# A streaming-encoder layer on one core: the second MLP product as seven half-size products, with weight sums made in DRAM

## The chip, the core and the metric

The kernel runs on one core of a Trainium2 chip. The engines are PE (matmuls), DVE, ACT and POOL (elementwise work, POOL only on SBUF) and SP, whose queue issues most transfers; sixteen DMA engines move the data of all queues. The metric is the time of one execution on the device in microseconds (us), as a median over runs.

## The reference, cut to what matters

One layer over 512 tokens and 16 meta tokens, width 1024, float32. The front computes an RWKV-7 branch and a forgetting-attention branch, gates them and projects the sum; then comes the MLP, which the change is about:

```python
h = h + (merged @ w_o[l]).astype(h.dtype)
z = rmsnorm(h, norm_mlp[l])
h = h + (jnp.square(jax.nn.relu(z @ w_up[l])) @ w_down[l]).astype(h.dtype)
return h[:, N_META:]
```

`z` is 512 x 1024 (the meta tokens are dropped by then), `w_up` 1024 x 4096, `w_down` 4096 x 1024.

## The kernel before

**Precision.** Every float32 operand of a large matmul is split into a high part (a cast to fp32r on ACT) and a low part (a subtraction, on DVE or POOL). A product is three passes: high by high, high by low, low by high (`passes`, line 259).

**Weights.** `load_h` (line 226) loads 128 x 512 floats, 256 KB, into a buffer `wraw` through SP's queue, casts it to `whi` on ACT (line 232) and subtracts to `wlo` (line 233). There are four buffers of each kind. `load_w` (line 236) is two such loads. The projections of the front have their own copy of this in `fetch` and `convert` (lines 430 and 438), with the subtraction on POOL (line 444).

**The front** (to about 450 us in the profile) is made of streams: the recurrence (`recurrent`, `chain`), attention, its features, and 40 projection blocks of u = rmsnorm(h) (`projections`, line 448). `Turns` (line 147) keeps a model of the time, `Clock`, and asks each stream in order of its rank for the time from which it can go on; the first that is due within `ROOM` of its rank writes its next instructions. This fixes the order on PE alone (`manual_schedule` at line 998). On the other engines and in the queues the compiler orders the instructions, by their place in the code and by when they are ready. Line 402, `act(gf, gf, AF.Tanh, scale=0.5)`, is one of the last steps before the streams start. The 16 gate blocks are projected at the lowest rank, written to DRAM (line 484) and read back at line 1028.

**The middle** (450 to 572 us): the output projections with the gates, `w_o`, the residual `hres` (4 blocks of 128 tokens by 1024), the second norm, and z transposed and split into `zhi` and `zlo`. The weights of the first two up blocks are loaded early into `we`, in the memory of `y_rw` and `y_fx`.

**The MLP** (from line 1106) goes over the 4096 hidden columns in two halves. In each half, 16 up blocks of 128 columns are computed: `up_part` writes 24 matmuls of 512 columns into a PSUM bank `po`, `up_evac` makes Relu on ACT (line 1122), squares on DVE (line 1124), casts to `fhi` (1125) and subtracts to `flo` (1126). The first three blocks of the first half are computed in two parts, since the tokens of z come in order. Then, for each half of the 1024 output columns, four banks `pd` gather 16 hidden blocks: every loaded block of `w_down` (128 x 512) serves four token blocks in three passes, 12 matmuls (line 1150). DVE adds each bank to `hres` (line 1153), and behind the second half the result is stored (line 1155).

Of the kernel before, what the change touches and what calls it, by code (L numbers as in the profile page):

```python
# [9 lines left out]
F32 = mybir.dt.float32  # L10
# [11 lines left out]
S = 512  # L22
# [3 lines left out]
HT = T // 2  # L26
KB = 8
CDEC = math.exp(-0.5)


C_MU = 0
# [28 lines left out]
class Clock:  # L60
# [35 lines left out]
    def read(self):  # L96

        new = self.nc.cur_bb.bb.instructions[self.seen:]
        self.seen += len(new)
        for x in new:  # L100
            outs = [o.bass_ap for o in x.outs if hasattr(o, "bass_ap")]
            ins = [o.bass_ap for o in x.ins if hasattr(o, "bass_ap")]
            if not outs:
                continue
            for o in outs:
                t = o.tensor
                if hasattr(t, "cap_key") and t.name not in self.free:
                    ring, n = self.rings.setdefault(str(t.cap_key).rsplit("_", 2)[0], []), t.tag_meta.bufs
                    self.free[t.name] = self.last(ring[-n]) if len(ring) >= n else 0.0
                    ring.append(t.name)  # L110
            names = [a.tensor.name for a in ins]
            out = outs[0].tensor.name
            eng = str(x.engine).split(".")[-1]

            def cols(a):
                return math.prod(n for _, n in a.ap[1:])
            deps = max([self.w.get(n, 0.0) for n in names] + [self.free.get(out, 0.0)])
            if eng == "PE":
                n = max(cols(outs[0]), 64)
# [27 lines left out]
class Turns:  # L147
# [37 lines left out]
def kernel(ctx, tc, ht, x, win, par, cst, gain, lora, wout, wo, wup, wdn, out, dbg=None):  # L185
# [73 lines left out]
    def passes(w, x):  # L259
        return ((w[0], x[0]), (w[0], x[1]), (w[1], x[0]))  # L260

    yp = ctx.enter_context(tc.tile_pool(name="yp", bufs=1))
    gates_d = [dr.tile([128, S], F32, name=f"gd{i}") for i in range(16)]

    with ExitStack() as st:
        up = st.enter_context(tc.tile_pool(name="up", bufs=1))
# [132 lines left out]

        lf, gf = (x[:, :T] for x in lfs)  # L400
        act(lf[:64], lf[:64], AF.Tanh)
        act(gf, gf, AF.Tanh, scale=0.5)
# [45 lines left out]
        def projections(total):  # L448
            fetched, done = None, 0
            while done < total:  # L450
                if fetched is None:
                    yield lambda: 0.0 if jobs else math.inf
                    fetched = fetch(jobs.pop(0))
                cur = convert(*fetched)
                fetched = fetch(jobs.pop(0)) if jobs else None
                while cur is not None:
                    (_, _, _, begin, parts, ev, need), w = cur
                    nxt = convert(*fetched) if fetched else None
                    fetched = fetch(jobs.pop(0)) if jobs else None
# [645 lines left out]

    with ExitStack() as st:
        dp = st.enter_context(tc.tile_pool(name="dp", bufs=1))
        for hh in range(2):
            fhi = dp.tile([128, 16, S], F32R, name="fhi")
            flo = dp.tile([128, 16, S], F32R, name="flo")  # L1110
            F = (fhi, flo)

            def up_part(w, po, t0, t1):
                n = 0
                for k in range(KB):
                    for a, b in passes(wk(w, k), Z):
                        mm(po[:, t0:t1], a, b[:, k, t0:t1], start=n == 0, stop=n == 23)  # L1117
                        n += 1

            def up_evac(b_, po):  # L1120
                r = dp.tile([128, 512], F32, name="r", bufs=2)
                act(r, po, AF.Relu)
                s2 = dp.tile([128, 512], F32, name="s2", bufs=2)
                V.scalar_tensor_tensor(s2, po, 0.0, r, ALU.max, ALU.mult)
                A.copy(fhi[:, b_, :], s2)
                V.tensor_tensor(flo[:, b_, :], s2, fhi[:, b_, :].bitcast(F32), ALU.subtract)

            first = 0
            if hh == 0:
# [4 lines left out]
                for b_ in range(3):  # L1134
                    up_part(ws[b_], pos[b_], 256, 512)
                    up_evac(b_, pos[b_])
                first = 3
            for b_ in range(first, 16):
                w = load_w(wup[16 * hh + b_])
                po = ppo()  # L1140
                up_part(w, po, 0, 512)
                up_evac(b_, po)
            for ch in range(2):
                pd = [ppd() for i in range(4)]
                for b2 in range(8):
                    w = load_w(wdn[hh, ch, b2])
                    for i, b1 in [(i, b1) for b1 in range(2) for i in range(4)] if b2 < 7 else [(i, b1) for i in range(4) for b1 in range(2)]:
                        b_ = 2 * b2 + b1
                        for n, (a, b) in enumerate(passes(F, w[b1])):
                            mm(pd[i], a[:, b_, 128 * i:128 * i + 128], b, start=b_ == 0 and n == 0, stop=b_ == 15 and n == 2)  # L1150
                for i in range(4):
                    hr = hres[:, i, 512 * ch:512 * ch + 512]
                    V.tensor_tensor(hr, hr, pd[i], ALU.add)
                    if hh == 1:
                        nc.sync.dma_start(out[128 * i:128 * i + 128, 512 * ch:512 * ch + 512], hr)


def host_layout(x, meta, norm_mix, w_in, b_gate, b_f, tm_mu, w0, w_lora_up, a0, a_lora_up, g_lora_up, k_k, k_a, r_k,
# [74 lines left out]
```

## Time and profile before

| | |
|---|---|
| median of 3 runs | 928.7 us (923.4 to 930.36) |
| span of the profiled execution | 921.7 us, 15446 instructions; its own time over all isn't listed beside the span |
| PE busy | 872.5 us (95%), mean granted clock 0.983 |
| DVE, ACT, POOL busy | 523.7 (57%), 424.9 (46%), 159.9 us (17%) |
| transfers | 83.30 MB, HBM read 75.99 MB, written 6.31 MB |

The span goes from the first to the last instruction. A busy PE is not PE at its peak, since matmuls overlap. In the lists of groups a row has the line, engine and operation, what is written from what, shape and count; then the busy time and the mean duration in ns of one; then the idle time of the engine just before, with what ended most of it. In a timeline a row begins with the start and the duration in us. A row of waits has who waited for whom, the total in us, how often, and the longest. A row of DMA issues ends with the KB of each and the median us from issue to landing.

### The profile page before, as it was taken

How to read it: one execution, taken by the hardware profiler on the slowest of the kernel's cores; microseconds unless marked ns; L12 is line 12 of the kernel's file. 1: busy time of each engine (PE TensorE's matmuls, PEld its weight loads, DVE VectorE, ACT ScalarE, POOL GpSimd, SP SyncE). 2: the span in 40 equal slices, each digit the busy share in tenths (PEclk: the TensorE clock that was granted, in tenths of full speed). 3: DMA queues.
4: the chain of work that ended last, by engine and by line, in shares of the span. 5: the costliest groups of instructions: out<-in, count | busy, mean ns of one | idle time of the engine just before them, and what ended most of it. 6: DMA issues, size and time to landing. Idle time of an engine off the chain costs nothing.

```text
span 921.7 us, 15446 instructions
## 1 busy us (share of the span) xinstructions
PE 872.5 (95%) x5964; PEld 709.4 (77%) x5964; DVE 523.7 (57%) x1052; ACT 424.9 (46%) x887; POOL 159.9 (17%) x145
## 2 busy tenths in 40 slices
PE   6589898999998999999989999999999999999998
PEld 4587785768896777676768878988888888888886
DVE  7966885465887893565387664454423245452322
ACT  7755352686465533674465553344322234442221
POOL 4253433123343352112102100000000000000000
PEclk9889998999999999999989999999999999999999
DMA  6121204022111142211266540132323232322331
GB/s 207 46 71 47 69 27 132 25 71 70 50 46 59 47 133 70 69 60 47 69 229 205 183 160 1 58 103 92 101 94 101 94 102 93 100 95 94 123 116 57
DMA packets 45449, 83.30 MB, mean 90 GB/s; under 512 B 5048, under 2 KB 6200, under 8 KB 45376
## 3 DMA queue, kind: packets, MB, share of 16 engines
q1 hardware_dynamic: 45376, 82.32, 26.8%
q8 instruction: 47, 0.77, 0.3%
q14 instruction: 26, 0.21, 0.1%
HBM read 75.99 MB, written 6.31 MB: 89 GB/s over the span
## 4 chain that ended last, share of the span: by engine, by line
PE 76%; DVE 15%; DMA 3%; ACT 3%; issue 2%; POOLq 0%; POOL 0%; SPq 0%; DVEq 0%; ACTq 0%
PE po L1117 19%; PE pd L1150 19%; PE pj L472 18%; PE po L1083 2%; PE po L1034 2%; PE pw L824 2%; PE psc L576 1%; PE py L621 1%; DVE tmp L806 1%; DMA wraw<-in_wup 1%; DVE AX L818 1%; DVE xt L373 1%; PE pbt L772 1%; DVE AX L807 1%; DMA wraw<-in_win 1%
## 5 line engine op out<-in xcount | busy, mean ns | idle before, releaser
L233 DVE TENSOR_TENSOR wlo<-wraw,whi 128x512 fp32r<-128x512 f32 x148 | 107.0, 724 | 171.6 <-ACT whi L232 170.1
L232 ACT CAST whi<-wraw 128x512 fp32r<-128x512 f32 x152 | 93.8, 620 | 190.4 <-PE pd L1150 109.6
L472 PE MATMUL pj<-uhi,whi 128*128 128x264 f32 (+1 forms) x480 | 168.5, 351 | 9.5 <-DVE orr L301 4.7
L472 PE MATMUL pj<-uhi,wlo 128*128 128x264 f32 (+1 forms) x480 | 156.3, 326 | 0.0
L472 PE MATMUL pj<-ulo,whi 128*128 128x264 f32 (+1 forms) x480 | 156.3, 326 | 0.0
L444 POOL TENSOR_TENSOR wlo<-wraw,whi 128x512 fp32r<-128x512 f32 x80 | 109.1, 1367 | 216.8 <-ACT whi L443 201.4
L472 PEld LDWEIGHTS pj<-uhi,whi 128*128 128x128 f32 x480 | 92.4, 192 | 30.6 <-issue 10.9
L1150 PE MATMUL pd<-whi,fhi 128*128 128x512 f32 x256 | 99.6, 389 | 0.0
L1150 PE MATMUL pd<-wlo,fhi 128*128 128x512 f32 x256 | 99.6, 389 | 0.0
L1150 PE MATMUL pd<-whi,flo 128*128 128x512 f32 x256 | 99.6, 389 | 0.0
L472 PEld LDWEIGHTS pj<-uhi,wlo 128*128 128x128 f32 x480 | 92.6, 193 | 7.2
L472 PEld LDWEIGHTS pj<-ulo,whi 128*128 128x128 f32 x480 | 92.7, 193 | 4.3
L1117 PE MATMUL po<-zhi,whi 128*128 128x512 f32 (+1 forms) x248 | 94.8, 382 | 0.0
L1117 PE MATMUL po<-zlo,whi 128*128 128x512 f32 (+1 forms) x248 | 94.8, 382 | 0.0
L1117 PE MATMUL po<-zhi,wlo 128*128 128x512 f32 (+1 forms) x248 | 94.8, 382 | 0.0
L443 ACT CAST whi<-wraw 128x512 fp32r<-128x512 f32 x80 | 49.4, 618 | 51.9 <-PE pj L472 27.5
L1150 PEld LDWEIGHTS pd<-whi,fhi 128*128 128x128 f32 x256 | 48.0, 188 | 10.1
L1150 PEld LDWEIGHTS pd<-wlo,fhi 128*128 128x128 f32 x256 | 48.0, 188 | 10.0
L1150 PEld LDWEIGHTS pd<-whi,flo 128*128 128x128 f32 x256 | 48.0, 188 | 9.9
L1117 PEld LDWEIGHTS po<-zlo,whi 128*128 128x128 f32 x248 | 46.6, 188 | 9.1
L1117 PEld LDWEIGHTS po<-zhi,whi 128*128 128x128 f32 x248 | 46.6, 188 | 9.0
L1117 PEld LDWEIGHTS po<-zhi,wlo 128*128 128x128 f32 x248 | 46.6, 188 | 9.0
(279 smaller groups left out, 1455.6 us busy)
## 6 DMA issues: line engine op xcount, KB each, us to landing
wraw<-in_win SPq DMA_DIRECT2D x84, 256.0 KB, 2.6
wraw<-in_wup SPq DMA_DIRECT2D x64, 256.0 KB, 2.6
wraw<-in_wdn SPq DMA_DIRECT2D x64, 256.0 KB, 2.6
gd<-gt SPq DMA_DIRECT2D x16, 256.0 KB, 2.1
wraw<-in_wout SPq DMA_DIRECT2D x16, 256.0 KB, 3.3
gl<-gd SPq DMA_DIRECT2D x16, 256.0 KB, 3.1
wraw<-in_wo SPq DMA_DIRECT2D x16, 256.0 KB, 3.2
xt<-in_ht SPq DMA_DIRECT2D x8, 264.0 KB, 4.7
```

Source lines behind the costliest of these rows:

```text
L232: A.copy(hi, raw)
L233: low.tensor_tensor(lo, raw, hi.bitcast(F32), ALU.subtract)
L373: V.scalar_tensor_tensor(xt[t][:, k, :], xt[t][:, k, :], pr[:, C_GN + k:C_GN + k + 1], rss[t], ALU.mult, ALU.mult)
L443: A.copy(hi, raw)
L444: G.tensor_tensor(lo, raw, hi.bitcast(F32), ALU.subtract)
L472: mm(po, a, b[:, k, a0:a1], start=n == 0, stop=n == 23)
L576: mm(sc, q[hs, 128 * i:128 * i + 128], k[hs, a:b], start=True, stop=True)
L824: mm(ps_[hs, n - b0, :], lhs(n)[hs], rhs(n)[hs], start=True, stop=True)
L1034: mm(po, a, b[:, k, :], start=n == 0, stop=n == 11)
L1083: mm(po, a[:, k, 128 * i:128 * i + 128], b[:, k, :], start=n == 0, stop=n == 23)
L1117: mm(po[:, t0:t1], a, b[:, k, t0:t1], start=n == 0, stop=n == 23)
L1150: mm(pd[i], a[:, b_, 128 * i:128 * i + 128], b, start=b_ == 0 and n == 0, stop=b_ == 15 and n == 2)
```

## The change

The second product F W (F: 512 x 4096, the squared Relu; W = `w_down`) is cut into 2 x 2 quadrants: F by token halves and by hidden blocks of even and odd number, W by those hidden blocks and by halves of the output columns. Strassen's scheme in Winograd's form computes it with seven products of quarter size in place of eight. It needs four sums of quadrants of F (s1 to s4), four of W, and sums of the results.

- The sums of W, `tsum`, four tensors of 2048 x 512 in DRAM, are made by DMAs: 16 copies of 1 MiB issued from ACT's queue and 16 adding DMAs of 1 MiB issued from POOL's. They are written as a new stream, `weight_sums`, of rank 9 in `Turns`, with due times of 50 us and 11 us more for each step; the copies are put behind line 402 (`opened`). `Clock` leaves them out of its model. t1 = B11 + B12, t3 = B12 + B22, t2 = B22 + t1, t4 = B21 + t2.
- The hidden dimension is worked through in three slices of 6, 6 and 4 pairs of blocks (`SLICES`). Up blocks are evacuated to a tile `R` in the memory of `y_rw` and `y_fx`; after each pair, POOL makes the four sums of 256 columns, and one cast and one subtraction of 7 x 256 columns make the pair's left factors.
- In each slice follow seven products. Each loads one 128 x 512 block per pair, from `wdn` or `tsum`, and uses it in 6 matmuls (two token blocks, three passes). Two products stay in PSUM over all slices (`x6`, `x7`, the four `pd` banks); two are gathered in SBUF (`v1`, `v5`); three are added to `hres` in each slice. In the last slice the sums over `v1`, `v5`, `x6`, `x7` follow on POOL and DVE.
- On the host, `w_down` is laid out in its four quadrants.

```diff
+SLICES = (6, 6, 4)
...
+            if out.startswith("tsum"):
+                continue
...
-    ROOM = {0: 0.0, 1: 0.8, 2: 1.5, 3: 1.5, 4: 2.5, 8: 0.5}
+    ROOM = {0: 0.0, 1: 0.8, 2: 1.5, 3: 1.5, 4: 2.5, 8: 0.5, 9: 0.0}
...
+    tsum = [dr.tile([2048, 512], F32, name=f"tsum{i}") for i in range(4)]
...
-        act(gf, gf, AF.Tanh, scale=0.5)
+        opened = act(gf, gf, AF.Tanh, scale=0.5)
...
+        def weight_sums():
+            def part(t, c):
+                return t[512 * c:512 * c + 512].rearrange("(a b) c -> a (b c)", b=4)
+            t1, t2, t3, t4 = tsum
+            b11, b12, b22, b21 = (wdn[i] for i in range(4))
+            steps = []
+            for c in range(4):
+                for dst, src in ((t1, b11), (t3, b12), (t2, b22), (t4, b21)):
+                    steps.append((dst, src, c, False))
+                for dst, src in ((t1, b12), (t3, b22), (t2, t1), (t4, t2)):
+                    steps.append((dst, src, c, True))
+            for n, (dst, src, c, adds) in enumerate(steps):
+                yield lambda: 50.0 + 11.0 * n
+                if adds:
+                    nc.gpsimd.dma_start(part(dst, c), part(src, c), accum_op=ALU.add, max_dma_last_dim=8192)
+                else:
+                    after(nc.scalar.dma_start(part(dst, c), part(src, c), max_dma_last_dim=8192), opened)
+        turns.add(9, weight_sums())
...
-        for hh in range(2):
-            fhi = dp.tile([128, 16, S], F32R, name="fhi")
...
+        def left_factors(fhi, flo, j, R):
+            a11, a12, a22, s1, s2, s3, s4, a21 = (R[:, i, :] for i in range(8))
+            G.tensor_tensor(s1, a22, a21, ALU.subtract)
+            G.tensor_tensor(s3, a11, a21, ALU.subtract)
+            G.tensor_tensor(s2, a11, s1, ALU.add)
+            G.tensor_tensor(s4, s2, a12, ALU.subtract)
+            A.copy(fhi[:, j], R[:, :7])
+            V.tensor_tensor(flo[:, j], R[:, :7], fhi[:, j].bitcast(F32), ALU.subtract)
...
+        for n_pairs in SLICES:
+            fhi = dp.tile([128, max(SLICES), 7, 256], F32R, name="fhi")
...
+            def product(x, left, right, start, stop):
+                for j in range(0, n_pairs, 2):
+                    r0 = 128 * (p0 + j)
+                    w = right_factors(right[r0:r0 + 256])
+                    final = left in (A12, S4, A22) and last and j == n_pairs - 2
+                    for i, b in [(i, b) for i in range(2) for b in range(2)] if final else [(i, b) for b in range(2) for i in range(2)]:
+                        for n, (a, c) in enumerate(passes((fhi, flo), w[b])):
+                            mm(x[i], a[:, j + b, left, 128 * i:128 * i + 128], c, ...)
...
+            gathered(v1, A11, B11)
+            product(x6, S2, T2, first, last)
+            product(x7, S3, T3, first, last)
...
+            gathered(v5, S1, T1)
...
+            added(0, 0, A12, B21, ALU.add)
+            added(0, 1, S4, B22, ALU.subtract)
+            added(1, 0, A22, T4, ALU.add)
...
-    wd = w_down[0].reshape(2, 8, 2, 128, 2, 512).transpose(0, 4, 1, 3, 2, 5).reshape(2, 2, 8, 128, 1024)
+    wd = w_down[0].reshape(16, 2, 128, 2, 512).transpose(1, 3, 0, 2, 4).reshape(4, 2048, 512)[[0, 1, 3, 2]]
```

More of the change, by code (lines that the diff above doesn't have):

```diff
@@ L1107, with up_part @@
         dp = st.enter_context(tc.tile_pool(name="dp", bufs=1))
-        for hh in range(2):
-            fhi = dp.tile([128, 16, S], F32R, name="fhi")
[L1110 to L1129, printed above, removed]
+        def up_part(w, po, t0, t1):
+            n = 0
+            for k in range(KB):
+                for a, b in passes(wk(w, k), Z):
+                    mm(po[:, t0:t1], a, b[:, k, t0:t1], start=n == 0, stop=n == 23)
+                    n += 1
@@ new lines, in right_factors @@
+        def right_factors(src):
+            return [load_h(src[128 * b:128 * b + 128], V, "w", (4, 4, 4)) for b in range(2)]
+        A11, A12, A22, S1, S2, S3, S4 = range(7)
+        B11, B22, B21, T1, T2, T3, T4 = wdn[0], wdn[2], wdn[3], *tsum
+        hr = [[hres[:, 2 * a:2 * a + 2, 512 * b:512 * b + 512] for b in range(2)] for a in range(2)]
+        v1, v5 = (dp.tile([128, 2, 512], F32, name=name) for name in ("v1", "v5"))
+        x6, x7 = ([ppd() for i in range(2)] for _ in range(2))
+        p0 = 0
@@ L1131 @@
+        for n_pairs in SLICES:
+            fhi = dp.tile([128, max(SLICES), 7, 256], F32R, name="fhi")
+            flo = dp.tile([128, max(SLICES), 7, 256], F32R, name="flo")
+            blocks = list(range(2 * p0, 2 * (p0 + n_pairs)))
+            held, R = [], None
+            if p0 == 0:
                 ws, pos = early + [load_w(wup[2])], [ppo() for i in range(3)]
@@ L1133 @@
                     up_part(w, po, 0, 256)
[L1134 to L1155, printed above, removed]
@@ new lines @@
+                held = list(zip(ws, pos))
+            for n, b_ in enumerate(blocks):
+                if held:
+                    w, po = held.pop(0)
+                    up_part(w, po, 256, 512)
+                else:
+                    w = load_w(wup[b_])
+                    po = ppo()
+                    up_part(w, po, 0, 512)
+                if n % 2 == 0:
+                    R = yp.tile([128, 8, 256], F32, name="R", tag=("y_rw", "y_fx")[n // 2 % 2])
+                    up_evac(po, R[:, 0:8:7, :])
+                else:
+                    up_evac(po, R[:, 1:3, :])
+                    left_factors(fhi, flo, n // 2, R)
@@ new lines @@
+            first, last = p0 == 0, p0 + n_pairs == 16
+            def product(x, left, right, start, stop):
[5 more added lines that the diff above has]
+                        for n, (a, c) in enumerate(passes((fhi, flo), w[b])):
+                            mm(x[i], a[:, j + b, left, 128 * i:128 * i + 128], c, start=start and j + b == 0 and n == 0,
+                               stop=stop and j + b == n_pairs - 1 and n == 2)
@@ new lines, in gathered, with added @@
+            def gathered(v, left, right):
+                x = [ppo() for i in range(2)]
+                product(x, left, right, True, True)
+                for i in range(2):
+                    if first:
+                        A.copy(v[:, i], x[i])
+                    else:
+                        V.tensor_tensor(v[:, i], v[:, i], x[i], ALU.add)
+            def added(a, b, left, right, op):
+                x = [ppo() for i in range(2)]
+                product(x, left, right, True, True)
+                for i in range(2):
+                    h = hr[a][b][:, i]
+                    V.tensor_tensor(h, h, x[i], op)
+                    if last:
+                        r0 = 256 * a + 128 * i
+                        nc.sync.dma_start(out[r0:r0 + 128, 512 * b:512 * b + 512], h)
@@ new lines @@
+            gathered(v1, A11, B11)
+            product(x6, S2, T2, first, last)
+            product(x7, S3, T3, first, last)
+            if last:
+                G.tensor_tensor(hr[0][0], hr[0][0], v1, ALU.add)
+                for i in range(2):
+                    V.tensor_tensor(v1[:, i], x6[i], v1[:, i], ALU.subtract)
+                G.tensor_tensor(hr[0][1], hr[0][1], v1, ALU.add)
+                for i in range(2):
+                    V.tensor_tensor(v1[:, i], v1[:, i], x7[i], ALU.subtract)
@@ new lines @@
+            gathered(v5, S1, T1)
+            if last:
+                G.tensor_tensor(hr[0][1], hr[0][1], v5, ALU.subtract)
+                G.tensor_tensor(hr[1][0], hr[1][0], v1, ALU.subtract)
+                for i in range(2):
+                    h = hr[1][1][:, i]
+                    V.tensor_tensor(h, h, v1[:, i], ALU.add)
+                    V.tensor_tensor(h, h, v5[:, i], ALU.subtract)
+                    r0 = 256 + 128 * i
+                    nc.sync.dma_start(out[r0:r0 + 128, 512:], h)
```

5 lines of the change are left out of this document (added).

## The prediction

> **What bounds the kernel now.** I read the page's sums first, then the chain that ended last, then a table of busy time by stage, the stages cut where the lines change.
>
> ```profile
> span 921.7 us, 15446 instructions
> ...
> PE 872.5 (95%) x5964; PEld 709.4 (77%) x5964; DVE 523.7 (57%) x1052; ACT 424.9 (46%) x887; POOL 159.9 (17%) x145
> ...
> q1 hardware_dynamic: 45376, 82.32, 26.8%
> ...
> PE 76%; DVE 15%; DMA 3%; ACT 3%; issue 2%; POOLq 0%; POOL 0%; SPq 0%; DVEq 0%; ACTq 0%
> ```
>
> ```profile
> core 0: us, PE busy (x) PEld busy (x) DVE busy (x) ACT busy (x) POOL busy (x), PEclk, DMA share, GB/s
> ...
> 35.00:100.00 65.00, 54.80 (x401) 47.63 (x402) 43.96 (x74) 38.78 (x70) 28.55 (x28) 0.89 0.18 61
> 100.00:200.00 100.00, 89.86 (x919) 71.04 (x918) 66.83 (x150) 50.13 (x114) 30.06 (x28) 0.95 0.18 59
> 200.00:300.00 100.00, 95.23 (x902) 80.36 (x901) 75.12 (x183) 58.51 (x145) 36.13 (x34) 1.00 0.18 60
> 300.00:400.00 100.00, 98.50 (x1014) 74.04 (x1014) 66.03 (x157) 47.61 (x122) 29.31 (x23) 1.00 0.26 85
> 400.00:450.00 50.00, 47.82 (x421) 37.65 (x422) 24.07 (x72) 27.22 (x65) 11.57 (x9) 1.00 0.11 38
> ...
> 572.00:917.00 345.00, 345.00 (x1579) 288.03 (x1578) 135.32 (x201) 111.06 (x185) 0.00 (x0) 1.00 0.28 93
> ```
>
> Two regimes. From 572 us on (the MLP) PE is busy for all of 345 us, DVE for 39% and ACT for 32%: there a matmul less is time less. Before 450 us (the front) PE is 84 to 98% busy, ACT around half, POOL around a third, and the DMA engines have over 70% of their time free. PE's order there is written out by hand, so it does not go round a late operand.
>
> **Part 1: seven products for eight.** The second MLP product has 768 matmuls of 512 columns; seven products of 96 are 672, so 96 go. Two matmuls 24 places apart give the pace:
>
> ```profile
> 912.00 0.39 PE L1150 MATMUL pd<-whi,flo 128*128 128x512 f32 x1
> ...
> 917.44 0.39 PE L1150 MATMUL pd<-whi,flo 128*128 128x512 f32 x1
> ```
>
> 5.44 / 24 = 0.227 us (the 0.39 is one matmul's own length; they overlap). 96 x 0.227 = 21.8 us off PE, in a stage where PE alone sets the time.
>
> **Part 2: more loads for fewer matmuls.** A block of right-hand weights now serves 6 matmuls instead of 12, one per 1.36 us, and 112 blocks are loaded, cast on ACT and subtracted on DVE instead of 64.
>
> ```profile
> L233 DVE TENSOR_TENSOR wlo<-wraw,whi 128x512 fp32r<-128x512 f32 x111 | 76.9, 693 | 158.0 <-ACT whi L232 156.7
> L232 ACT CAST whi<-wraw 128x512 fp32r<-128x512 f32 x111 | 69.1, 623 | 177.5 <-PE pd L1150 103.3 <-PE po L1117 58.7 <-DVE hres L1153 12.4
> ```
>
> ```profile
> 526.53 9.72 SPq L1069 DMA_DIRECT2D wraw<-in_wo  x8
> 536.58 3.25 SPq L229 DMA_DIRECT2D wraw<-in_wup  x3
> ```
>
> ACT needs 0.62 and DVE 0.69 of each 1.36 us, and the casts today wait for PE, not for loads. The closest sight of four load buffers going round with nothing else to wait for is line 1069: eight loads in 536.58 - 526.53 = 10.05 us, 1.26 each. That is 8% under what PE will ask, so the loads keep up, barely. Bounds: 0, and 16 us if a round takes 6.0 instead of 5.05 us (landing 0.7 later, as line 229's wout loads do at 3.3 against 2.6 us, and one 0.25 us collision): 112 x (1.50 - 1.36). I take 1.5 us, nearer the row.
>
> ```profile
> wraw<-in_wdn SPq DMA_DIRECT2D x64, 256.0 KB, 2.6
> ...
> wraw<-in_wout SPq DMA_DIRECT2D x16, 256.0 KB, 3.3
> ```
>
> **Part 3: the end of each slice.** The first product needs the last pair's seven left factors. Behind the last up block come Relu, square, three dependent POOL operations of 256 columns, a cast of 1792 columns and a subtraction of 1792. For the first two an up block of now, which ended at 651.1, where the next began:
>
> ```profile
> 651.11 0.39 PE L1117 MATMUL po<-zhi,whi 128*128 128x512 f32 x1
> ...
> 651.65 0.59 ACT L1122 ACTIVATE r<-po 128x512 f32<-128x512 f32 x1
> ...
> 652.39 0.68 DVE L1124 SCALAR_TENSOR_TENSOR s<-po,r 128x512 f32<-128x512 f32 x1
> ```
>
> ```profile
> L444 POOL TENSOR_TENSOR wlo<-wraw,whi 128x512 fp32r<-128x512 f32 x80 | 109.1, 1367 | 216.8 <-ACT whi L443 201.4 <-PE psc L576 10.1 <-PE py L621 4.4
> ```
>
> To 653.1 that is 2.0 us; POOL at half of 1367 ns, three times, with a handover of 0.15 each (652.24 to 652.39): 2.5; the cast 1.4 to 2.2 us (0.62 times 3.5 at most, less by the fixed part), taken 1.6; then the subtraction 2.1 to 2.4. High parts are there 6.2 us after the block, low parts 8.5. Six pairs put 30 matmuls, 6.8 us, ahead of the last pair, its low part 0.45 later: 1.2 us of stall, twice. Four pairs put 18, 4.1 us: about 4 us, once. Sum 6.4; zero if PE takes the next product's first matmuls meanwhile; I take 5. The left factors themselves (per pair of 10.9 us: four POOL operations, 2.7; ACT and DVE under 7 each) lie beside the up matmuls. The extra sums into hres and v1 are 128x512 operations of 0.69 us on DVE, two per product of 8.2 us, beside matmuls. The end is the same two evacuations and two stores behind the last matmul.
>
> MLP in all: -21.8 + 1.5 + 5 = -15 us.
>
> **Part 4: the weight sums in the front.** 16 copies (ACT's queue) and 16 adds (POOL's queue) of 1 MiB each, DRAM to DRAM. No row shows a transfer with both ends in DRAM or an adding one. Loads moved 82.32 MB in 26.8% of 921.7 us, 333 GB/s if all engines are busy: 3.1 us per MiB for one pass, the lower bound. Upper: every pass over DRAM counted, two for a copy (6.3), three for an add (9.4). I take the upper ends, since a load, the nearest row, has one end there: 101 + 151 = 252 us of all engines. The stages from 35 to 450 us use 79 us of 415 now, so the volume fits. The Trainium skill (DMA: Bandwidth & Descriptors, Latency and other measured facts) gives 207 to 214 GB/s for copies between HBM tensors, so by it a copy would take an estimated 4.9 us and the copies 78 in place of 101. By the Trainium skill's fit for transfers that POOL issues (same page, Anatomy of one DMA), 2.0 us plus bytes over 436 GB/s, an add would take an estimated 4.4 us, 70 us for all. No row here can check either; by both the sums would ask 148 instead of 252 us, and the waits below would shrink to some 0.6 of what I take.
>
> So volume is not the price; the queues are. First, when do they run? The planner's due times (50 us, then every 11) only place the copies in the code. The queues of the other engines are not in code order:
>
> ```profile
> 0.82 0.40 DVE L877 MEMSET uv<- 64x128 f32 x2 [0.82 <-PEq L1222]
> ```
>
> ```profile
> 50.58 0.35 ACT L899 ACTIVATE SP<-uv,pend 64x64 f32<-64x64 f32 x1 [0.57 <-DVE pend L692]
> ```
>
> ```profile
> L883 PE MATMUL pch<-uv,L x144: 222/222/271, 183.3 to 428.2; 128*64 128x64 f32 x144
> ```
>
> ```profile
> 465.05 2.23 SPq L1047 DMA_DIRECT2D hres<-in_x  x4
> ...
> 500.33 0.38 SPq L229 DMA_DIRECT2D wraw<-in_wout  x1
> ```
>
> Lines 877 and 899 belong to the chain whose first matmul is at 183 us and ran at 0.8 and 50.6; line 1047 stands behind the whole wout loop and was issued 35 us before its last load. Whatever waits for nothing goes into the first idle place. The copies wait for nothing but line 402:
>
> ```profile
> 34.93 0.64 ACT L402 ACTIVATE lf<-lf 128x528 f32<-128x528 f32 x1
> ```
>
> So I expect most of the 16 copies in ACT's gaps soon after 35.6 us, in a bunch, and the adds as soon as their copies are thought to be down. Such an instruction stands at the head of an in-order queue until its wait ends:
>
> ```profile
> ACT lw L256 <- DMA lraw<-in_lora: 20.4, 7, 6.7
> SPq L1069 <- DMA wraw<-in_wo: 2.6, 2, 1.5
> ACT whi L443 <- DMA wraw<-in_win: 8.5, 6, 2.9
> SPq L434 <- POOL wlo L444: 206.3, 52, 13.5
> ```
>
> ACT has stood 6.7 us for one late load already; SP has waited for the landing of earlier loads before issuing another, as the loads take a few completion counters in turn (eight in the compiled program); and the weight pipeline hangs on POOL (line 444) before the next load. Priced:
>
> Issue: an SP issue of line 1047 takes about 0.43 us (2.23 for four, less one longer); 16 on ACT are 7 us; on POOL between that and a POOL conversion (1.37 us), 7 to 22. ACT is half idle, POOL two thirds: I put 6 us on the path; bounds 0 and 29.
>
> Waits on ACT and SP: with copies of 6.3 us in a bunch and eight counters, copy 9 waits for copy 1, copy 16 for copy 8, at 35 + 8 x 6.3 = 85 us. ACT has 60% of these 50 us filled with its own work (38.78 of 65), 30 us. Behind a waiting copy stand evacuations of pj (two buffers) and casts, and PE waits for those. Bounds 0 (copies spread out) and 30; I take half, 15.
>
> Waits on POOL: eight of the adds take another add's sum. Standing at the head for a 9.4 us add and its landing is 11.5 us, 92 in all at most; POOL is idle two thirds of the time, leaving 30; the four raw and four converted buffers ahead of PE take more than half of that. I take 12; bounds 0 and 30.
>
> Front: +33 us, bounds 0 and 89. Cover gone nowhere else: the sums are needed at about 640 us and are down well before.
>
> **Sum.** 921.7 - 15 + 33 = 939.7 us of span. What lies around the span of the profiled execution isn't listed; the median of the runs is 7.0 us over it (the runs 1.7 to 8.7), so I add 7: **947 us**.
>
> **Rivals.**
>
> Hidden sums, faster. If the copies keep the due times, a step every 11 us against 6.3 to 9.4 us of transfer, no queue waits long, and the front pays part of the issue, 4 us: 921.7 - 15 + 4 + 7 = 918, and 910 if the slice ends and loads cost 2 instead of 6.5 and the front 1. For: 70% of the DMA engines' time is free, and ACT waited only 8.5 us for all loads of the front. Against: the three rows above on order.
>
> The front paced by the DMA queue, slower by more. Its place is POOL's queue; if each add is queued where its sources were expected at 3.1 us per pass but the engines need 252 + 79 us for everything from 35 us on, the last add is done at 366 us, against 35 + 100 + 79 = 214 by the lower price, and POOL trails by what its buffers don't take. It decides once the adds need more than their spacing. Half of the 152 us: 921.7 - 15 + 76 + 7 = 990. For: adds have three passes. Against: once POOL is late, its own work no longer fills the gap, so part is counted twice.
>
> Loads bound the products. At 1.50 us a block the gain of part 1 shrinks by 16; with the hidden front: 921.7 - 21.8 + 16 + 5 + 4 + 7 = 932, no change that shows. For: the 8% margin of line 1069. Against: that row had 8 loads on top of other traffic, at 1.26 us.
>
> The change may also not do what it says: PE would keep about 0.227 us a matmul but 672 of them might not be reached at once, if POOL's left factors were slower beside DVE; the 10.9 us per pair against 2.7 makes that too unlikely for a chance of its own.
>
> **How the numbers follow.** Forecast 0.42, hidden sums 0.36, paced front 0.12, load-bound products 0.10. A measurement here tells about 1%, 9.3 us, from no change. Faster by over 1% (under 919.4): 0.32 of the hidden case and 0.02 of the load-bound one, 0.34. Within 1%: 0.04, 0.08 and 0.02 of the forecast, 0.14. Slower: 0.40 + 0.12 = 0.52. The range for 8 in 10 goes from 910, the hidden case at its best, to 985, just under the paced front; the forecast's own range is 932 to 970 (front +18 to +56).
>
> **What would show it.** Right: copies on ACT within some 30 us after line 402's second activation; ACT and SP rows waiting for DMA of tsum; POOL rows of line 444 behind adds; PE's idle share from 35 to 300 us up by about 30 us; the stage from the first up matmul to the end near 330 us instead of 345; 0.227 us between matmuls; gaps of PE behind the last up block of a slice. Wrong: copies 10 us apart on ACT over 300 us; no idle time on PE beyond today's in the front; then the kernel is faster. In the MLP, ACT casts waiting for DMA wraw instead of PE would mean that the loads bound it.

## The result, and the profile after

The changed kernel takes 956.53 us (median of 4 runs, 955.41 to 960.95) against 928.77 us before on the same chip: ratio 1.0314 [1.0257, 1.037], slower. The forecast was 947.0 us, so its sign holds and its size is 9.5 us short: the change costs 27.8 us where 18.3 were forecast.

The page of the changed kernel first: span, engines, the two queues of the sums (packets, MB, share of 16 engines), and the issues of the new transfers (KB of each, median us to landing).

```profile
span 955.6 us, 15670 instructions
...
PE 866.4 (91%) x5868; PEld 700.5 (73%) x5868; DVE 590.1 (62%) x1102; ACT 460.1 (48%) x923; POOL 238.3 (25%) x229
...
q0 software_dynamic: 2304, 16.78, 9.0%
q10 hardware_dynamic: 2304, 16.78, 4.7%
...
tsum<-in_wdn ACTq DMA_DIRECT2D x16, 1024.0 KB, 9.4
...
tsum<-in_wdn POOLq DMA_DIRECT2D x8, 1024.0 KB, 17.7
tsum<-tsum POOLq DMA_DIRECT2D x8, 1024.0 KB, 12.5
```

There are 96 matmuls fewer (5964 to 5868), as the scheme says, yet PE is busy only 6.1 us less, and its idle time grew. The copies run in q10, the adds in q0: 4.7% of 955.6 us is 45 us of all sixteen engines, 2.8 per copy; 9.0% is 86 us, 5.4 per add.

Where the span grew is read from first and last starts. These rows come from the view of one line's instructions, of the kernel before (lines 1117 and 1150) and after (lines 887, 1138 and 1204); the last two figures ahead of the semicolon are the first and last start.

```profile
L1117 PE MATMUL po<-zlo,we x32: 278/283/285, 567.5 to 582.7; 128*128 128x256 f32 x32
...
L1150 PE MATMUL pd<-whi,fhi x256: 389/389/389, 656.5 to 917.0; 128*128 128x512 f32 x128
```

```profile
L887 PEld LDWEIGHTS pch<-uv,L x144: 132/138/138, 225.1 to 470.2; 128*64 128x64 f32 x144
...
L1138 PE MATMUL po<-zlo,we x32: 278/283/285, 610.3 to 625.5; 128*128 128x256 f32 x32
...
L1204 PE MATMUL po<-whi,fhi x160: 387/389/501, 677.6 to 950.9; 128*128 128x512 f32 x160
```

The first up matmuls moved from 567.5 to 610.3: 42.8 us lost ahead of the MLP. From there to the last matmul it is 340.6 us instead of 349.5: 8.9 gained. And the first matmul of the chain moved from 183.3 to 225.1, so nearly all of the loss lies before 225 us. Busy time by stage, after:

```profile
35.00:100.00 65.00, 48.62 (x327) 41.02 (x328) 40.94 (x66) 32.09 (x60) 24.14 (x28) 0.84 0.89 241
100.00:200.00 100.00, 70.65 (x487) 58.42 (x489) 51.49 (x98) 26.15 (x56) 35.39 (x35) 0.81 0.95 251
200.00:300.00 100.00, 94.15 (x1132) 76.45 (x1129) 64.53 (x171) 64.43 (x155) 27.43 (x29) 0.98 0.19 62
```

From 35 to 200 us PE falls from 84 and 90% busy to 75 and 71%, the granted clock from 0.89 and 0.95 to 0.84 and 0.81, and the DMA engines go from 0.18 to 0.89 and 0.95. Behind 200 us the front looks as before. The 32 sums, seen by their tile (issues of the changed kernel, first and last start):

```profile
L1017 ACTq DMA_DIRECT2D tsum<-in_wdn x16: 497/497/621, 34.6 to 179.3; - x16
L1015 POOL DMA_DIRECT2D tsum<-in_wdn x8: 805/976/1384, 40.4 to 160.8; - x8
L1015 POOL DMA_DIRECT2D tsum<-tsum x8: 805/819/833, 68.7 to 192.6; - x8
```

The due times put the last one 341 us behind the first; they all went within 158. Who stood waiting (total us, times, longest):

```profile
POOL tsum L1015 <- DMA tsum<-in_wdn: 34.1, 6, 10.9
...
ACT whi L447 <- DMA wraw<-in_win: 30.4, 13, 6.5
...
POOL tsum L1015 <- DMA tsum<-tsum: 29.1, 4, 15.8
...
ACT lw L259 <- DMA lraw<-in_lora: 27.8, 7, 14.4
...
PE pj L476 <- POOL wlo L448: 17.2, 2, 14.2
```

POOL stood 63.2 us at the head of its queue ahead of adds. ACT waited 30.4 us for the front's weight loads, 8.5 before. One of POOL's stretches in the timeline, with a cast of ACT ahead of it (start, duration, and in brackets the idle time before):

```profile
135.26 0.66 ACT L447 CAST whi<-wraw 128x512 fp32r<-128x512 f32 x1
...
157.19 0.81 POOL L1015 DMA_DIRECT2D tsum<-tsum  x1 [15.81 <-DMA tsum<-tsum]
...
157.79 1.54 POOL L448 TENSOR_TENSOR wlo<-wraw,whi 128x512 fp32r<-128x512 f32 x1
```

For 15.81 us POOL has nothing before it but an add that waits for another add's landing. The weight conversion of line 448 starts 0.6 us after the start of that add's issue. Counting casts and conversions in order, it is the one whose cast is shown, so it had lain ready for almost 22 us; before, no conversion lay ready for 2 us. PE waited for such a conversion for up to 14.2 us at a time. Before, no row had PE waiting for line 444.

### The profile page after: what moved, and what is told of

Read it like the earlier page. It is cut to its first block, busy times and chain, and to the rows that moved or that the text cites. A ratio compares the mean times of both kernels' runs of the same rounds, so it can differ in the third digit from the quotient of the medians.

```text
span 955.6 us, 15670 instructions
## 1 busy us (share of the span) xinstructions
PE 866.4 (91%) x5868; PEld 700.5 (73%) x5868; DVE 590.1 (62%) x1102; ACT 460.1 (48%) x923; POOL 238.3 (25%) x229
## 3 DMA queue, kind: packets, MB, share of 16 engines
q0 software_dynamic: 2304, 16.78, 9.0%
q10 hardware_dynamic: 2304, 16.78, 4.7%
## 4 chain that ended last, share of the span: by engine, by line
PE 61%; DVE 14%; DMA 12%; ACT 5%; issue 4%; POOL 2%; SPq 0%; ACTq 0%; DVEq 0%; POOLq 0%
PE po L1138 18%; PE pj L476 14%; PE po L1204 8%; PE pd L1204 3%; DMA tsum<-in_wdn 3%; DMA wraw<-in_win 3%; PE po L1108 2%; PE po L1059 2%; DMA tsum<-tsum 2%; DVE tmp L810 1%; DVE wlo L236 1%; PE py L625 1%; PE psc L580 1%; PE pw L828 1%; DVE xt L377 1%
## 5 line engine op out<-in xcount | busy, mean ns | idle before, releaser
L236 DVE TENSOR_TENSOR wlo<-wraw,whi 128x512 fp32r<-128x512 f32 x196 | 150.8, 784 | 82.5 <-ACT whi L235 82.2
L235 ACT CAST whi<-wraw 128x512 fp32r<-128x512 f32 x200 | 122.7, 620 | 143.7 <-PE po L1138 58.7
L476 PE MATMUL pj<-uhi,whi 128*128 128x264 f32 (+1 forms) x480 | 172.5, 359 | 15.9 <-ACT gt L487 9.0
L476 PE MATMUL pj<-uhi,wlo 128*128 128x264 f32 (+1 forms) x480 | 159.9, 333 | 17.2 <-POOL wlo L448 17.2
L447 ACT CAST whi<-wraw 128x512 fp32r<-128x512 f32 x80 | 49.0, 618 | 64.9 <-DMA wraw<-in_win 30.4
L1151 POOL TENSOR_TENSOR R<-R 128x256 f32<-128x256 f32 x16 | 16.7, 1044 | 240.7 <-DVE R L1145 240.7
L1204 PE MATMUL po<-wlo,fhi 128*128 128x512 f32 x160 | 62.8, 393 | 5.9 <-DVE wlo L236 5.8
L1204 PE MATMUL po<-whi,fhi 128*128 128x512 f32 x160 | 62.3, 391 | 2.0 <-ACT fhi L1154 1.8
L1204 PE MATMUL po<-whi,flo 128*128 128x512 f32 x160 | 62.1, 389 | 0.0
L1155 DVE TENSOR_TENSOR flo<-R,fhi 128x1792 fp32r<-128x1792 f32 x16 | 32.4, 2026 | 43.4 <-ACT fhi L1154 43.4
L1154 ACT CAST fhi<-R 128x1792 fp32r<-128x1792 f32 x16 | 27.1, 1696 | 29.7 <-POOL R L1153 29.7
## 6 DMA issues: line engine op xcount, KB each, us to landing
tsum<-tsum POOLq DMA_DIRECT2D x8, 1024.0 KB, 12.5
```

What stands on the lines that cost most here:

```text
L235: A.copy(hi, raw)
L236: low.tensor_tensor(lo, raw, hi.bitcast(F32), ALU.subtract)
L447: A.copy(hi, raw)
L1151: G.tensor_tensor(s3, a11, a21, ALU.subtract)
L1154: A.copy(fhi[:, j], R[:, :7])
L1155: V.tensor_tensor(flo[:, j], R[:, :7], fhi[:, j].bitcast(F32), ALU.subtract)
```

## The experiments

All ratios are against the kernel before on the same chip. A ratio is turned into us by 928.7. By the intervals, a difference of two ratios is known to some 4 to 6 us.

**1. The changed kernel without the sums.** The products read plain quadrants of W in their place; values differ, work does not.

```diff
-        turns.add(9, weight_sums())
-        B11, B22, B21, T1, T2, T3, T4 = wdn[0], wdn[2], wdn[3], *tsum
+        B11, B22, B21, T1, T2, T3, T4 = wdn[0], wdn[2], wdn[3], wdn[1], wdn[0], wdn[2], wdn[3]
```

> The changed kernel without the weight sums: the copies and adds are left out, and the products that would read a sum read a plain quadrant of w_down of the same size instead. Theory (the loss is all in the front, by the sums): the front is as before and the MLP keeps what the traces show, 42.8 us late at its start against 33.9 us late at the end, so 9 us faster than before: 920 us. Rival (the seven products cost something in the front too, or reading the sums is what slows the products): 930 us or more, or, if reading plain quadrants is quicker, 912.

923.37 us, ratio 0.991 [0.9876, 0.9945]: 8.4 us faster than before. The seven products are worth that, and the sums cost 0.0404 x 928.7 = 37.5 us. That is the quantity the next runs divide.

**2. The sums alone.** The kernel before, with the stream of 32 transfers added and nobody reading the sums.

```diff
+        opened = act(gf, gf, AF.Tanh, scale=0.5)
...
+        turns.add(9, weight_sums())
```

> The kernel before with the sums added to its front, same stream, rank and due times, and nobody reads them; its MLP is as before. Theory (the loss sits in the front and is independent of the products): 928.8 + 42 = 971. Rival (the order of the front that the planner writes, or the loads' clock, came with the products): 940 to 955.

970.91 us, ratio 1.0432 [1.0377, 1.0487]: +40.1 us. The loss belongs to the sums, not to anything in the products, and the two parts add up: 40.1 - 8.4 = 31.7 against 29.2 measured together.

**3. The copies alone.** The adds are left out.

```diff
                 if adds:
+                    continue
+                if adds:
                     nc.gpsimd.dma_start(part(dst, c), part(src, c), accum_op=ALU.add, max_dma_last_dim=8192)
```

> The changed kernel with the 16 copies where they are and the 16 adds left out (the sums are then plain copies). Theory (most of the loss is POOL standing at the adds, 63 us in its rows of waits, and the adds' share of the engines): the copies alone cost 8 to 15 us in the front, 928 to 935. Rival (copies alone fill the engines and hold ACT and the loads): 20 us or more, 940 and over.

922.69 us, ratio 0.9938 [0.9907, 0.9969]: 2.6 us over the kernel without sums, within the two intervals. Both expectations were too high. From 100 to 200 us the copies load the DMA engines (0.46, 0.18 before), and PE is no less busy than before (stage of the copies-only kernel; PE was 89.86 before):

```profile
100.00:200.00 100.00, 92.40 (x943) 74.98 (x941) 66.98 (x150) 50.54 (x116) 33.02 (x29) 0.95 0.46 147
```

**4. Plain copies in place of the adds,** from POOL's queue, with the same waits. The sums hold other values.

```diff
-                    nc.gpsimd.dma_start(part(dst, c), part(src, c), accum_op=ALU.add, max_dma_last_dim=8192)
+                    nc.gpsimd.dma_start(part(dst, c), part(src, c), max_dma_last_dim=8192)
```

> The changed kernel with the 16 adding transfers as plain copies from the same queue, with the same waits between them (the sums are then wrong values of the same size). Theory (an adding transfer keeps the engines longer, 0.60 us a packet of 8 KB against 0.31 for the plain copies in this trace, and the waits of POOL follow from that): the engines are freed some 40 us earlier and POOL stands half as long, 935 to 942. Rival (it is the waits in order on POOL that cost, whatever moves): 950 or more.

933.83 us, ratio 1.004 [1.0008, 1.0073]. So 16 more transfers with their waits are worth 9.5 us over the copies alone, and making them add another 25.4 us. POOL's queue on the page, then POOL's waits and PE's wait for POOL's conversions:

```profile
q0 software_dynamic: 2304, 16.78, 4.8%
```

```profile
POOL tsum L1015 <- DMA tsum<-in_wdn: 31.0, 9, 6.5
...
POOL tsum L1015 <- DMA tsum<-tsum: 12.6, 1, 12.6
...
PE pj L476 <- POOL wlo L448: 5.7, 2, 4.4
```

The same packets and bytes take 4.8% of 931.3 us, 45 us; adding takes 86. POOL's waits are 43.6 instead of 63.2 us, and PE's wait for its conversions is 5.7 instead of 17.2. This run changes two things at once, the engines' time and the waits that follow from it; the next ones part them.

**5. Every transfer in its place.** The stream gets the first rank, and each copy and add is tied behind the last instruction of its own queue at its place in the code, so that the order of the code is the order in the queues.

```diff
+                tc.add_manual_dep(x.ins, prev.name, ..., reason="in its place")
...
-        turns.add(9, weight_sums())
+        turns.add(-1, weight_sums())
```

> The changed kernel with the sums held in their place: the stream has the first rank instead of the last, so a step is written when its due time of 50 + 11 n us comes, and each copy and add is put behind the instruction that its own queue had last at that place. Theory (queues: the sums are bunched between 35 and 195 us and what waits in order behind them pays): spread over 350 us they find their sources landed and the loads beside them have room, the front loses 4 to 12 us in place of 42, so 924 to 932. Rival (volume: the front pays for the bytes whenever they move): 950 or more.

943.42 us, ratio 1.0138 [1.0092, 1.0184], between the two expectations: 16.3 us better than the changed kernel, 21.2 worse than without sums. The copies now run from 90 to 419 us, the adds from 140 to 465, yet waits are left:

```profile
POOL tsum L1021 <- DMA tsum<-tsum: 12.9, 3, 8.5
...
POOL tsum L1021 <- DMA tsum<-in_wdn: 10.8, 1, 10.8
```

An add still followed closely on the transfer that it needs, so pacing alone was a test of half of the theory. But in this run no row has PE waiting for line 448; ACT waits 35.4 us for `lraw` loads, 20.3 without sums. What the 11.4 us over the next experiment are made of is not shown.

**6. Late adds.** Copies about 7 us apart from the start of the streams, the adds about 15 us apart, and in such an order that each one's sources were written at least four adds earlier.

```diff
+            turns.add(-1, paced(nc.scalar, ..., lambda n: 20.0 + 7.0 * n,
+                                ((t1, b11), (t3, b12), (t2, b22), (t4, b21))))
+            turns.add(-1, paced(nc.gpsimd, ..., lambda n: 140.0 + 15.5 * n,
+                                ((t1, b12), (t3, b22), (t2, t1), (t4, t2)), accum_op=ALU.add))
```

> The changed kernel with the same 16 copies and 16 adds, but no instruction of a queue may wait for a late one: copies on ACT in their place in the code about 7 us apart from the start of the streams, adds on POOL pinned about 15 us apart from some 190 us on, all adds of raw weights first, so that an add's sources were written four or more adds earlier. Theory (what the adds cost is POOL standing at the head of its queue for a late transfer, and the front's loads behind a bunch): POOL waits for tsum under 5 us, first chain matmul near 185 us, last pj near 470 us, and 924 to 933 us, a few us over the kernel without sums (923). Rival (adding traffic takes the front's time by itself, through slower small loads and the 0.8 us that POOL spends on each issue): waits gone as well, but 940 or more, like the paced kernel before (943).

930.57 us, ratio 1.0015 [0.9991, 1.0039], in the theory's range: 27.8 us of the 37.5 are gone with the same 32 transfers. The tile's view, with its section on what the issues waited for:

```profile
L1018 POOL DMA_DIRECT2D tsum<-in_wdn x8: 791/818/971, 103.2 to 296.9; - x8
L1018 POOL DMA_DIRECT2D tsum<-tsum x8: 793/808/817, 319.6 to 431.6; - x8
its engine sat idle before it (us, times) until:
who waited for it (us, times):
```

Nothing stands under "sat idle before it": the 63.2 us are 0. The first adds went earlier than meant, at 103 us. The run changes the waits and the bunch together, so the 27.8 us belong to both. It is the best version that makes all sums, and it is not faster than the kernel before.

**7. Late plain copies,** the same kernel with copies for adds (other values in the sums).

```diff
-                                ((t1, b12), (t3, b22), (t2, t1), (t4, t2)), accum_op=ALU.add))
+                                ((t1, b12), (t3, b22), (t2, t1), (t4, t2))))
```

> As the kernel with late adds, but each add is a plain copy to the same place, from the same queue, so that the sums hold other values. Theory (waits): with no waits left, whether the transfers add or copy makes no difference over 4 us; 923 to 931 us. Rival (the adding traffic itself): the plain version is at least 8 us faster than the adding one.

921.22 us, ratio 0.9924 [0.9894, 0.9955]: 1.3 us over the kernel without sums, and 8.5 us (by the ratios) under the late adds. So here the rival was right: without any wait for `tsum`, adding still costs what copying doesn't. Waits of the two from 190 to 475 us (ACT) and 290 to 475 us (PE), the late adds first:

```profile
ACT lw L259 <- DMA lraw<-in_lora: 14.6, 3, 9.2
...
PE pj L476 <- ACT vf L539: 5.1, 1, 5.1
```

```profile
ACT lw L259 <- DMA lraw<-in_lora: 9.8, 3, 6.3
...
PE pj L476 <- ACT vf L539: 2.2, 1, 2.2
```

A 64 KB load that is issued 2 us behind an add holds ACT for 9.2 us, and 6.3 behind a copy; PE then waits 5.1 and 2.2 us for an evacuation. That is a part of the 8.5 us, not most of it. Both kernels have the same order on PE, so their profiled executions can be compared matmul by matmul. The one with adds ends 12.5 us later; 6.2 of these are there at 293 us already and 8.8 at 326, and by 351 us this load has made them 12.9. The 2.6 us between 293 and 326 come without a longer wait: near 304 us PE waits 2.31 us for an operand in one and 2.32 in the other, and behind it the granted clock is 0.50 with adds and 1.00 with copies (the last three figures of a row are clock, DMA share and GB/s):

```profile
304.00:310.00 6.00, 6.00 (x34) 5.40 (x36) 2.13 (x4) 3.11 (x5) 1.28 (x1) 0.50 0.33 101
```

```profile
298.00:304.00 6.00, 5.84 (x50) 4.60 (x50) 4.27 (x8) 4.11 (x7) 1.28 (x1) 1.00 0.14 46
```

The profiled execution with adds is also the longest of its twelve runs (934.42). So the 8.5 us stand by the timed runs, and how they come about stays open.

**8. Sums written by short rows,** meant to test whether the size of a packet matters.

```diff
-                return t[512 * c:512 * c + 512].rearrange("(a b) c -> a (b c)", b=4)
+                return t[512 * c:512 * c + 512]
```

> The changed kernel with the copies and adds in rows of 2 KB in place of 8 KB; bytes, queues and order as they are. Theory (the engines change between queues packet by packet, so a weight load or a 64 KB load waits for a packet of 0.3 or 0.6 us of the sums at each of its own packets; smaller packets let it through): the loads of the front land near 3 us again and the front loses 10 to 15 us less, 940 to 946. Rival (the engines' time for the sums counts, and small rows do not shorten it): 955 to 965.

1002.54 us, ratio 1.0792 [1.0737, 1.0847], worse than either expectation. It does not answer its question, since the page shows the same packets as ever on either queue (2304 for 16.78 MB):

```profile
q0 software_dynamic: 2304, 16.78, 8.5%
```

The rows were merged. What did change is how the transfers fell together: PE is 41% busy at clock 0.69 from 100 to 200 us (first row), and POOL waits 59.4 + 48.5 = 107.9 us for sums.

```profile
100.00:200.00 100.00, 40.59 (x256) 32.59 (x253) 21.36 (x35) 22.24 (x40) 26.40 (x27) 0.69 0.82 201
```

```profile
POOL tsum L1015 <- DMA tsum<-in_wdn: 59.4, 8, 20.0
...
PE pj L476 <- POOL wlo L448: 58.6, 6, 25.1
POOL tsum L1015 <- DMA tsum<-tsum: 48.5, 4, 23.7
...
ACT L688 <- DMA tsum<-in_wdn: 17.8, 1, 17.8
```

The engine time is as before, and the kernel takes 44 us more than the changed one; PE's wait for POOL's conversions grew by 41.4 us, from 17.2 to 58.6. Here ACT, too, stood 17.8 us at a copy that waited for an earlier copy's landing. Why the same bytes bunched more stays open.

**9. Three quarters of the sums in the MLP,** pinned to the up blocks of each slice, where POOL is nearly idle.

```diff
+            for n, step in enumerate(sum_steps(0)):
+                yield lambda: (60.0, 75.0, 90.0, 105.0, 140.0, 170.0, 220.0, 270.0)[n]
...
+                    if n == ((0, 0, 1, 1, 3, 4, 6, 8) if p0 < 12 else (0, 0, 1, 1, 2, 3, 5, 6))[m]:
+                        make_sum(*step)
```

> The changed kernel with three quarters of the sums moved out of the front: the first quarter of the rows is summed in the front at due times 15 to 50 us apart, each next quarter while the up blocks of one slice are computed, each step behind the last instruction of its queue at that place. Theory (the front pays because its queues have no slack, the up blocks have 9 us of it per load): the front loses 3 to 6 us, the MLP nothing, 922 to 926. Rival (the adds hold POOL and the loads in the MLP as well, and left factors or weights come late): 930 or more.

941.24 us, ratio 1.013 [1.0086, 1.0174]; the rival's outcome. The front is as without sums (the first up matmul at 575.9 us, 576.7 without sums), but the MLP takes 20 us more, as it has no slack for late loads:

```profile
ACT whi L235 <- DMA wraw<-in_wup: 28.4, 8, 7.9
```

```profile
628.28 0.50 PE L1141 MATMUL po<-zhi,wlo 128*128 128x512 f32 x1 [1.53 <-DVE wlo L236]
...
629.38 0.63 PE L1141 MATMUL po<-zhi,whi 128*128 128x512 f32 x1
...
631.94 0.63 PE L1141 MATMUL po<-zhi,whi 128*128 128x512 f32 x1
```

After the gap of 1.53 us, the second within 2.3 us, the matmuls slow: from 629.38 to 631.94 there are seven, of which the last starts six places on, 2.56 / 6 = 0.43 us apart instead of 0.227.

**10. The short slice first,** without sums (4, 6, 6 pairs), a single run.

```diff
-SLICES = (6, 6, 4)
+SLICES = (4, 6, 6)
```

> The kernel without sums (products read plain quadrants) with slices of 4, 6 and 6 pairs in place of 6, 6 and 4. Theory (the short last slice is where the MLP stalls: 30 matmuls ahead of the last pair's factors instead of 18, and POOL's and DVE's closing sums spread over longer products): from the first transpose to the last matmul 353 to 355 us in place of 357.5. Rival (the stalls belong to the closing sums alone, or move to the first slice): 357 to 358.

921.95 us in one run; the MLP is 0.4 us shorter, 357.1 us from the first transpose to the last matmul, the rival's outcome. PE's waits from 570 us on were 7.4 us without sums with the slices of the change, and are 7.9 with the short slice first: the wait for the left factors (1.8) moved with the short slice from 878 to 628 us, and the waits for DVE's weight subtractions stayed (5.6 and 6.1).

## Why the prediction was right in sign and 9.5 us short

The forecast was a gain of PE time in the MLP, eaten by queues in the front. That is what happened. By its own terms, in the profiled executions: the front cost 42.8 instead of 33 (+9.8), the MLP gave 8.9 instead of 15 (+6.1), and 0.9 instead of 7 us lay between span and median (-6.1). The timed runs divide it better: the sums cost 37.5 instead of 33 us (+4.5), the products gave 8.4 instead of 15 (+6.6).

**The 7 us around the span was a misreading.** The profiled execution of the changed kernel took 957.5 us for a span of 955.6, so 1.9 us lie around a span. Before's 7.0 were mostly that its profiled execution was a quick one. The terms found by timed runs, -8.4 for the products and +37.5 for the sums, do not depend on it; a difference of a few us between the fronts of two single profiles should not be read.

**Seven products for eight (-21.8): held.** 5868 matmuls are left and their pace is unchanged. **Loads (+1.5): nothing measured.** ACT waits 21.7 us for `tsum` loads over the whole MLP, but no PE wait ends on them, and between the slice ends (690 to 800 us and 815 to 905) PE keeps 0.227 us a matmul. **Slice ends (+5, sum 6.4): too small.** Counting by the starts how far PE fell behind 0.227 us a matmul, they are 12.8 us: 2.1, 2.1 and 8.6. -21.8 + 12.8 = -9.0, which is the 8.9 measured. The working had 1.2, 1.2 and 4. For the first two it named the right operations but not who comes behind them. Of the 8.6, the last pair's left factors are 2.1; the other 6.5 are an item that it did not count. End of slice one, then three rows of slice three:

```profile
684.13 2.03 DVE L1155 TENSOR_TENSOR flo<-R,fhi 128x1792 fp32r<-128x1792 f32 x1 [3.17 <-ACT fhi L1154]
...
686.81 0.50 PE L1204 MATMUL po<-wlo,fhi 128*128 128x512 f32 x1 [1.41 <-DVE wlo L236]
```

```profile
934.81 2.68 POOL L1238 TENSOR_TENSOR hres<-hres,v 128x1024 f32<-128x1024 f32 x1 [4.90 <-DVE v L1214]
935.19 2.84 DVE L1243 TENSOR_TENSOR hres<-hres,v 128x512 f32<-128x512 f32 x1
...
938.69 0.50 PE L1204 MATMUL po<-wlo,fhi 128*128 128x512 f32 x1 [2.68 <-DVE wlo L236]
```

PE does not wait for the left factors at 686.81 but for the next weights, whose subtraction stood behind the 2.03 us one on DVE. In slice three the closing sums on DVE and POOL delay those subtractions again. The row at 935.19 is a DVE operation that elsewhere takes 0.69 us; beside a POOL operation it took 2.84 and ended 0.54 us behind it. POOL's other three closing sums did the same to weight subtractions, which started at 915.73, 921.98 and 927.85 and took 2.4 to 2.9 us. "The end is the same two evacuations and two stores" was the step that failed.

**Queue order: held in substance, off in extent.** The due times did not hold on the queues, as rows 877, 899 and 1047 suggested. But "within some 30 us" was wrong: the copies took from 34.6 to 179.3, strung out between ACT's own late work.

**Price of a transfer (252 us of all engines): too high, 131 measured.** One pass, 3.1 us, was called the lower bound of a copy, which took 2.8. Its duration is another matter: with the transfers spread out (experiment 6) a copy landed in 5.6 us, an add in 8.5 to 10.1, near the 6.3 and 9.4 that were taken. The durations came out right, though no run shows that passes over DRAM are what sets them; the step to "of all engines" was wrong. The estimates worked out in the prediction from the Trainium skill (DMA: Bandwidth & Descriptors, Latency and other measured facts and Anatomy of one DMA) came out at 78 + 70 = 148, nearer in sum; but copies needed 45 and adds 86, and no run here shows an adding transfer at the price of a plain one. Taken as durations they were 4.9 us for a copy, near the 5.6 measured, and 4.4 for an add, half of what was measured.

**Waits on ACT and SP (15): far too high.** The copies cost 2.6 us with issue and all. No row has ACT or SP waiting for a transfer of `tsum` in the front. The wait that was priced exists, but only where the copies bunched closer: in experiment 8 the copy that was issued at 107.72 had waited for one that landed at 107.70. **Issue (6): too high;** 32 issues and plain transfers with no wait cost 1.3 us (experiment 7), not to be told from nothing.

**Waits on POOL (12, bounds 0 to 30): the term that was mis-sized.** POOL stood 63.2 us, two thirds of the 92 that the working had as its utmost; removing the waits and the bunch took 27.8 us back. They were discounted for POOL's idle time and for the buffers ahead of PE, but behind the wait of 15.81 us PE had none left. POOL's own standing is not the measure: in experiment 4 it stood 43.6 us, and the 16 transfers cost 9.5. PE's wait for its conversions is nearer: none in experiment 3, 5.7 us in 4, 17.2 in the changed kernel and 58.6 in 8, which are 2.6, 12.1, 37.5 and 81.9 us over the kernel without sums. The rest is not divided between late loads on ACT and the lower clock. And one term was absent: adding costs another 8.5 us without any wait at POOL.

So the 37.5 us are 1.3 for traffic and issue, 8.5 for adding when spread out, and 27.8 for transfers that stand in each other's way. The forecast's 33 were 6 + 15 + 12. That 33 came near 37.5 is luck: two terms were 20 us too high together, one was 16 too low and one was missing. The hidden-sums rival, 918 us, is what plain copies reach (921); no version with adding transfers came near it.

## What to carry to other kernels

A transfer issued from a computing engine's queue costs above all what its wait holds up: 16 plain copies that waited for nothing late cost 2.6 us here, within the noise. Before adding one, ask what it must wait for, and put it in the queue only where that is long done, with an explicit tie if the compiler orders the queue. Price an adding transfer by itself; here it cost more than a plain one even without a wait. A dependency between two transfers on such a queue should have several others in between. And when an algorithm saves matmuls at the price of sums, list every sum at the end of the last stage with what stands behind it on its engine: here a saving of 21.8 us on PE was 8.4 before the sums of W were even made.

## What the hardware showed that was not expected

- An adding transfer from DRAM to DRAM holds the DMA engines about twice as long as a plain one of the same packets: 5.4 against 2.8 us of all sixteen per MiB (9.0% of 955.6 us against 4.8% of 931.3).
- A load of 64 KB is held up behind 1 MiB transfers: ACT's longest wait for one was 14.4 us after, 6.7 before.
- A gap can cost PE more than its length, but need not. After 1.53 us without a matmul the next ones ran 0.43 us apart for 2.6 us or more (experiment 9), while after the gap of 2.68 us at the end of the changed kernel (938.69) they kept 0.23. After equal waits of 2.3 us the clock was 0.50 in one execution and 1.00 in another (experiment 7). In the stages where PE idled most the granted clock was lowest: 0.81 at 71% busy, 0.69 at 41% (experiment 8).
- A DVE operation of 0.69 us took 2.4 to 2.9 us beside a POOL operation of 2.4 to 2.8 us, and ended some 0.55 us behind it, four times out of four in the last slice of the changed kernel.
